# Gate-unit splitting of four more weight groups in a transformer layer, kept in DRAM as two parts and loaded as operands

## The chip, the cores and the metric

One NeuronCore of a Trainium2 chip runs the whole layer as one program. The metric is device time in microseconds from launch to end, lower is better. The kernel before ran three times: 2187.90, 2187.95 and 2191.87 us, median 2187.95.

## The reference

One layer of a decoder trunk, all in float32, sequence 1024, width 1024:

```
x = x + 1/2 * SwiGLU_1(RMSNorm(x))
z = RMSNorm(x) @ W_in           # u, v, c_q, c_kv, k_rope, q_mem, gates A, B, C
A: u * (tril(W_s) layernorm(v) + b), in chunks of 128
B: causal attention, 8 heads; q = rmsnorm(c_q) @ w_uq, k and v = rmsnorm(c_kv) @ w_ukv
C: cross-attention to 256 memory tokens, 4 heads
x = x + (sum_i sigmoid(gate_i) * (y_i @ W_branch_i)) @ W_out
x = x + 1/2 * SwiGLU_2(RMSNorm(x))
```

`w_uq` is 384 x 768, `w_ukv` 256 x 1024, each `W_branch` 512 x 1024.

## The kernel before, in words

**Three products for one.** TensorE takes its operands in a reduced form of float32 (`F32R`). To keep the accuracy, every operand x is split into two parts, hi = x rounded to that form and lo = x - hi, and `mm3` (L145) multiplies hi by hi, hi by lo and lo by hi into one PSUM bank. The split (`split`, L133) is a copy on ScalarE (L134) and a subtraction on VectorE (L135). Every weight that is fetched raw goes through it once before it can be used; `load` and `convert` (L103, L107) do this for a fetched weight in pieces of 512 columns: the DMA brings the raw weight into a `raw` buffer (three of them, each 128 x 1024), and the split writes it into a pair of `whi` and `wlo` buffers (five of each).

**The stages.** First feed-forward; the gates' product h @ W_in (`Gates.run`, L1767); the mixer (`mixer`, L926: spatial gating, memory attention, up-projections, causal attention); then branch B, the output projection and the second feed-forward.

**The gates.** W_in is worked off in 19 units, each a seven-product Strassen scheme of 7 x 4 x 3 = 84 matmuls of 512 columns. A unit fetches one quad of weight tiles (`fetch`, L1415: two DMAs of 512 KB, and two buffers for the sums that VectorE builds, L1422), splits them (`weights`, L1436), keeps the first product as p1 (a ScalarE copy, L1483), and writes its outputs to DRAM. The buffers come from two pools: ten `x4` and eleven `w4`, each 128 x 1024 floats; units with an even number take four `x4`, units with an odd number two `x4` and two `w4` from unit 3 on. Between units other weights are already prepared: after units 4 to 7 the sums of W_out (`out_sums`, L1687), which go to DRAM as hi and lo parts and are later loaded as operands (the same is done for the memory's keys and values after unit 8, and for the memory query in units 14 and 15). `out_sums` takes the four buffers of the next turn, two loads, four GpSimd subtractions (L1696 to L1699), one split and three stores.

**The mixer.** Value rows (`value_rows`, L571) are multiplied with W_v, whose four pairs of wide buffers stay in use until the last row. `gating` (L620) mixes them, `mem_attention` (L711) and branch A's output product (`branches`, L550) interleave with it. `latent` (L430) reads the latent rows through `raw`. `qkv` (L450) then multiplies with w_uq and w_ukv, interleaved with steps of branch C, and `attention` (L789) begins with the rest of branch C. `branches` takes one weight per 128 output columns: 128 x 4 x 128 floats, 256 KB, loaded raw and split by one copy and one subtraction of 512 columns. Branch A's parts go to a `whi` and a `wlo` buffer, branch C's into halves of one `raw` buffer (`half_pair`, L546), so that branch C holds one `raw` buffer to stage and one for the parts; for its last two weights VectorE does the copy too. `qkv` loads w_uq in three fetches and w_ukv in two; together they hold all five pairs of wide buffers.

**The order.** All DMAs around the change are issued by SyncE (SP) in one queue, in order: a transfer whose buffer or operand is not ready holds all behind it. In the gates TensorE's order is written out by hand for the first units and kept as the program has it for the rest; SP, ScalarE, VectorE and GpSimd are ordered by a planner that simulates the timeline and assigns the buffers. In the mixer the planner orders TensorE as well. The last keys and queries of the causal attention go to DRAM (L530, L533) and come back as pairs (`pair_half`, L539) before TensorE can transpose them (L406).

Of the kernel before, what the change touches and what calls it, by code (L numbers as in the profile page):

```python
# [9 lines left out]
F32 = mybir.dt.float32  # L10
F32R = mybir.dt.float32r
# [3 lines left out]
ALU = mybir.AluOpType  # L15
AXX = mybir.AxisListType.X

P = 128
D = 1024
S = 1024  # L20
DT = D // P
# [5 lines left out]
H = 8  # L27
NOPE = 64
ROPE = 32
QK = NOPE + ROPE  # L30
VD = 64
QR = 384
# [13 lines left out]
MEM_AT = 8  # L46
# [3 lines left out]
class Kernel:  # L50
# [399 lines left out]
    def qkv(self, cq, ckv, krs, krr, eps, rc, aside):  # L450


        nc, a, tc = self.nc, self.a, self.tc
        half = ROPE // 2
        wq = self.load(a["mla_w_uq"])
        wk = [self.load(a["mla_w_ukv"][g]) for g in range(2)]
        T = 2
        vv = []
        with tc.tile_pool(name="qkvp", bufs=2) as p:
# [16 lines left out]
            for i0 in range(0, NT, T):  # L476
                q = p.tile([P, T, H, QK], F32, name="q")
                k = p.tile([P, T, H, QK], F32, name="k")
                ss = self.stat("qk_ss", 2 * T * H).rearrange("p (a t h) -> p a t h", a=2, t=T)
                for t in range(T):  # L480
                    i = i0 + t
                    c = slice(i * P, i * P + P)
# [60 lines left out]
            eng.dma_start(t, d[h // 2][:, half * NT // 2:(half + 1) * NT // 2])  # L543
            self.pair[n, half] = t

    def half_pair(self):  # L546
        t = self.raw(F32R)
        return t[:, :512], t[:, 512:]

    def branches(self, br, yt, sink, halves, rooms=(), first=3):  # L550

        nc, a, w, rooms = self.nc, self.a, {}, list(rooms)

        steps = [(dt, hf) for hf in halves for dt in range(first)]
        for dt, hf in steps + [(dt, hf) for dt in range(first, DT) for hf in halves]:
            if dt not in w:
                w[dt] = self.load(
                    a["w_branch"][br, dt], rooms.pop(0) if rooms else None,
                    copy=nc.vector.tensor_copy if br == 2 and dt >= DT - 2 else None)
            sig = self.row()  # L560
            nc.sync.dma_start(sig, self.sig[br * DT + dt][:, hf])
            b = self.bank()
            self.branch(b, w[dt], yt, hf)
            sink(dt, hf, sig, b)
            yield
# [360 lines left out]
    def mixer(self, norm):  # L926
        nc, tc, a = self.nc, self.tc, self.a
        dt = lambda shape, n: self.dram.tile(shape, F32, name=n)
        self.pair = {}
        self.qd = dt([H // 2, P, NT, 2 * QK], "qd")  # L930
        self.kd = dt([H // 2, P, NT, 2 * QK], "kd")
        md, mc = dt([DT, 2, P, 512], "md"), dt([DT, 2, P, 512], "mc")
        pairs = lambda n: [tuple(x[:, i] for x in norm.op[n][p]) for p in range(2) for i in range(2)]
        h = [pairs("b12") + pairs("b22"), pairs("b11") + pairs("b21")]

        def sink_a(d, f, sig, ps):
            nc.vector.tensor_tensor(sig, sig, ps, op=ALU.mult)
            nc.sync.dma_start(md[d, f], sig)

        def sink_c(d, f, sig, ps):  # L940
            m = self.row()
            nc.sync.dma_start(m, md[d, f])
            nc.vector.tensor_tensor(sig, sig, ps, op=ALU.mult)
            nc.gpsimd.tensor_tensor(sig, sig, m, op=ALU.add)
            nc.sync.dma_start(mc[d, f], sig)

        ln_g, ln_b = self.row(), self.row()
        nc.sync.dma_start(ln_g, a["sg_ln_g"].partition_broadcast(P))
        nc.sync.dma_start(ln_b, a["sg_ln_b"].partition_broadcast(P))
        with tc.tile_pool(name="mem", bufs=1) as p:  # L950
            w = self.convert(self.w_v)
            kt, vv = self.mem_operands(p)
            qt, nr, query = self.mem_query(p)
            query(0)
            vs = [[], []]
            sw = self.gating_weights()
            ya, aside = self.gating(sw, vs)
            branch_a = self.branches(0, ya, sink_a, (1, 0), first=4)
            fill, mix = (lambda x=x: next(x) for x in (branch_a, aside))
            for f, q, also in ((1, 0, {}), (1, 1, {}), (0, 0, {}), (0, 1, {d: mix for d in (1, 2, 4, 6, 7)})):  # L960
                x = self.value_rows(f, q, h, w, also)
                self.value_norm(x, q, ln_g, ln_b, vs[f])
            lead = [(fill, fill), (fill, mix, mix), (mix, fill), (mix, mix, fill)]
            branch_c = self.mem_attention(
                kt, vv, qt, nr, query, lead, branch_a, lambda yc: self.branches(
                    2, yc, sink_c, (0, 1), [self.half_pair] * DT, first=1))
        with tc.tile_pool(name="pairs", bufs=1) as self.pairs:
            with tc.tile_pool(name="lt", bufs=1) as self.lp:
                z = self.latent()
                for _ in range(2):  # L970
                    next(branch_c)
                vv = self.qkv(*z, branch_c)
            yb = self.attention(vv, branch_c)
        return yb, mc
# [335 lines left out]
class OpNorm:  # L1310
# [45 lines left out]
    def part(self, p):  # L1356
        for piece in self.pieces(p):
            piece()
# [34 lines left out]
class Seven:  # L1393
# [42 lines left out]
    def weights(self, f, part):  # L1436

        k = self.k
        a1, a2, sa, sb = self.quad[f]
        src, names = {  # L1440
            "a": (a1, ("a11", "a12")), "s": (sa, ("s2", "s1")), "t": (sb, ("s3", "s4")),
            "l": (a2[:, :1], ("a22",))}[part]
        n = len(names)
        hi, lo = (k.wide(x).rearrange("p (a w) -> p a w", a=2)[:, :n] for x in ("whi", "wlo"))
        k.split(hi, lo, src)
        return {x: (hi[:, i], lo[:, i]) for i, x in enumerate(names)}
# [166 lines left out]
class Gates(Seven):  # L1613
# [73 lines left out]
    def out_sums(self, u, rooms):  # L1687
# [15 lines left out]
        nc.sync.dma_start(k.wo["hi", q][:, :, i], a1)  # L1703
        nc.sync.dma_start(k.wo["lo", q][:, :, i], a2)

    def square_sums(self, n, half, d):

        k = self.k
        sq = k.row()
        self.nc.scalar.activation(sq, d, ACT.Square)  # L1710
        fresh = self.bank is None
        if fresh:
            self.bank = k.bank()

        def go():
            for t in range(4 * half, 4 * half + 4):
                at = t * MH + n - QM
                self.nc.tensor.matmul(
                    self.bank[:, at:at + 1], sq[:, t % 4 * P:t % 4 * P + P], k.ones,
                    start=fresh and t == 4 * half, stop=True, skip_group_check=True)  # L1720

        self.sums_todo.append(go)
# [44 lines left out]
    def run(self, x1d, r0):  # L1767


        k, norm, x4, w4 = self.k, self.norm, self.k.x4, self.w4  # L1770
        last = UNITS - 1
        k.mkv = {n: [k.dram.tile([P, D], F32, name=f"{n}{i}") for i in range(2)] for n in ("mk", "mv")}
        k.wo = {
            (n, q): k.dram.tile([P, 2, 2, 512], F32, name=f"wo_{n}{q}") for n in ("sum", "hi", "lo") for q in range(2)}
        k.zsums = k.const.tile([P, NT * MH], F32, name="zsums")
        k.g_mq = k.const.tile([P, 1], F32, name="g_mq")
        k.after(self.nc.vector.tensor_scalar(k.g_mq, k.mq_g, -(MD ** -0.5), None, op0=ALU.mult), k.last)
        E = mybir.EngineType
        with k.tc.manual_schedule(engines={E.PE, E.DVE, E.Activation}):
            self.units((0, 1), extra=2, kinds=(k.bank, k.single, k.single, k.bank, k.bank), late=1, turn=2)  # L1780
        with k.tc.manual_schedule(engines={E.PE}):
            for f in range(3, last + 1):
                self.fetch(f, [x4, w4, x4, w4] if (last - f) % 2 else [x4] * 4)
                if f == last:
                    more = k.fetch(k.a["w_v"], [x4, x4])
                    k.w_v = chain([next(more) for _ in range(2)], more)
                    for p in range(2):
                        norm.t.t[0, p] = w4()
                        self.nc.sync.dma_start(norm.t.t[0, p], x1d[0, p])
                    norm.s[0] = k.norm_scale(r0)  # L1790
                    for p in range(2):
                        norm.norm(0, p)
                self.unit(f)
                turn = [x4, w4, x4, w4], [x4] * 4
                if MEM_AT > f >= MEM_AT - 4:
                    self.out_sums(f - MEM_AT + 4, turn[(last - f + 1) % 2])
                if f == MEM_AT:
                    self.memory(turn[(last - f) % 2] + turn[(last - f + 1) % 2])
                if 2 * f >= CQ and self.bank is not None:
                    self.flush()  # L1800
                    nc = self.nc
                    nc.vector.tensor_copy(k.zsums, self.bank[:, :NT * MH])
                    self.bank = None
            for p in range(2):
                norm.put("b12", p, norm.t.t[0, p])
# [425 lines left out]
```

## Time and profile before

| | |
|---|---|
| median of three runs | 2187.95 us (2187.90 to 2191.87) |
| profiled execution, first to last instruction (span) | 2187.2 us; what lies around it was not recorded apart, the median of the runs is 0.75 us above it |
| TensorE busy | 2163.2 us (99%), 10153 matmuls |
| VectorE, ScalarE, GpSimd busy | 1560.4 (71%), 908.5 (42%), 219.0 us (10%) |
| DMA | 315.8 MB, mean 144 GB/s |
| granted TensorE clock | 1.00 over the span |
| gates' units 3 to 18 | about 700 to 1056 us |
| mixer up to the causal attention | about 1036 to 1290 us |

A row of a group names the line, the engine, the operation, the tiles written and read, the count, the busy time and the mean of one in ns; what follows the second bar is the idle time ahead of it and what ended it. In a row by stage each engine's busy time has its instruction count behind it. Many matmuls overlap, so busy TensorE means that it never ran dry, not that it ran at its peak.

### The profile page before, as it was taken

Reading aid. Unit: us, or ns where it says so; the run is one execution under the profiler, and the core shown is the slowest. Engines: PE = TensorE matmul, PEld = TensorE weight load, DVE = VectorE, ACT = ScalarE, POOL = GpSimd, SP = SyncE. Lnnn points to the kernel's source line nnn. Section 1 sums busy time; section 2 is a strip of 40 time slices with the busy share of each in tenths; the row PEclk is TensorE's granted clock in tenths of the full one; section 3 lists DMA queues with packets and bytes.
Section 4 is the critical chain, followed back from the end, with each engine's and each line's share of the span. In section 5 each row is a group of like instructions: output and inputs, shape, how many; then the busy total and the mean of one; then the engine's idle time right before and its main releaser. Section 6 shows DMA issues by size and latency. Waiting matters only on the chain.

```text
span 2187.2 us, 27190 instructions
## 1 busy us (share of the span) xinstructions
PE 2163.2 (99%) x10153; PEld 1797.6 (82%) x10153; DVE 1560.4 (71%) x2285; ACT 908.5 (42%) x1375; POOL 219.0 (10%) x234
## 2 busy tenths in 40 slices
PE   8999999999999999999999999999999999999999
PEld 4788888888888888888888889988888888888887
DVE  7965666569889657556588788898985665556964
ACT  5432223233445435433266549844532322224332
POOL 0011212110000220000000431200001111211000
PEclk9999999999999999999999999999999999999999
DMA  4232333384432673334356661166243333338442
GB/s 155 88 124 91 112 101 114 107 329 151 151 125 81 227 260 106 135 135 170 118 173 198 207 202 35 54 229 238 82 135 96 97 115 92 116 130 317 140 140 97
DMA packets 131925, 315.80 MB, mean 144 GB/s; under 512 B 14608, under 2 KB 23056, under 8 KB 131792
## 3 DMA queue, kind: packets, MB, share of 16 engines
q1 hardware_dynamic: 129392, 311.69, 42.6%
q10 hardware_dynamic: 2400, 2.36, 0.3%
q8 instruction: 80, 1.31, 0.3%
q14 instruction: 53, 0.43, 0.1%
HBM read 216.35 MB, written 97.65 MB: 144 GB/s over the span
## 4 chain that ended last, share of the span: by engine, by line
PE 87%; DVE 9%; DMA 2%; ACT 1%; issue 1%; POOL 0%; SPq 0%; ACTq 0%; DVEq 0%; POOLq 0%
PE one L148 15%; PE one L150 15%; PE one L149 15%; PE bank L148 10%; PE bank L149 10%; PE bank L150 10%; PE mm L148 2%; DVE wlo L135 2%; PE mm L150 2%; PE mm L149 2%; PE bank L864 1%; PE bank L879 1%; DVE h L135 1%; PE bank L880 1%; PE bank L406 1%
## 5 line engine op out<-in xcount | busy, mean ns | idle before, releaser
L134 ACT CAST whi<-x 128x1024 fp32r<-128x1024 f32 (+1 forms) x213 | 200.5, 946 | 510.4 <-PE one L149 213.1
L1457 DVE TENSOR_TENSOR t<-t,one 128x512 f32<-128x512 f32 x149 | 102.3, 687 | 245.0 <-PE one L150 244.8
L135 DVE TENSOR_TENSOR wlo<-x,whi 128x1024 fp32r<-128x1024 f32 (+1 forms) x213 | 233.3, 1099 | 42.5 <-ACT whi L134 42.5
L148 PE MATMUL bank<-h,whi 128*128 128x512 f32 x592 | 231.1, 391 | 1.1 <-ACT t L1483 0.7
L149 PE MATMUL bank<-h,whi 128*128 128x512 f32 x592 | 230.5, 389 | 0.0
L150 PE MATMUL bank<-h,wlo 128*128 128x512 f32 x592 | 230.4, 390 | 0.0
L135 DVE TENSOR_TENSOR wlo<-w,whi 128x1024 fp32r<-128x1024 f32 (+1 forms) x153 | 168.8, 1117 | 75.3 <-ACT whi L134 75.1
L134 ACT CAST whi<-w 128x1024 fp32r<-128x1024 f32 (+1 forms) x153 | 142.4, 954 | 167.0 <-PE one L149 104.9
L148 PE MATMUL one<-h,whi 128*128 128x512 f32 x528 | 206.6, 391 | 1.7 <-ACT t L1483 1.2
L150 PE MATMUL one<-h,wlo 128*128 128x512 f32 x528 | 205.6, 389 | 0.5 <-DVE wlo L135 0.5
L149 PE MATMUL one<-h,whi 128*128 128x512 f32 x528 | 205.5, 389 | 0.0
L148 PE MATMUL one<-w,whi 128*128 128x512 f32 x464 | 180.7, 390 | 0.3 <-DVE t L1457 0.3
L150 PE MATMUL one<-w,wlo 128*128 128x512 f32 x464 | 180.6, 389 | 0.0
L1971 POOL TENSOR_TENSOR raw<-raw 128x512 f32<-128x512 f32 x36 | 75.6, 2100 | 882.5 <-DVE raw L1829 652.2
L1457 DVE TENSOR_TENSOR raw<-t,one 128x512 f32<-128x512 f32 x130 | 89.1, 686 | 88.1 <-PE one L150 81.1
L149 PE MATMUL one<-w,whi 128*128 128x512 f32 x380 | 147.9, 389 | 0.0
L148 PE MATMUL one<-whi 128*128 128x512 f32 (+1 forms) x371 | 143.9, 388 | 0.0
L149 PE MATMUL one<-wlo,whi 128*128 128x512 f32 (+1 forms) x371 | 143.7, 387 | 0.0
L150 PE MATMUL one<-whi,wlo 128*128 128x512 f32 (+1 forms) x371 | 143.7, 387 | 0.0
L148 PEld LDWEIGHTS bank<-h,whi 128*128 128x128 f32 x592 | 111.1, 188 | 24.6 <-ACT t L1483 1.2
L150 PEld LDWEIGHTS bank<-h,wlo 128*128 128x128 f32 x592 | 111.1, 188 | 23.2
L149 PEld LDWEIGHTS bank<-h,whi 128*128 128x128 f32 x592 | 111.2, 188 | 22.7
(424 smaller groups left out, 4784.8 us busy)
## 6 DMA issues: line engine op xcount, KB each, us to landing
x<-in_ffn_w_gu_dram SPq DMA_DIRECT2D x76, 512.0 KB, 4.4
w<-tdt SPq DMA_DIRECT2D x40, 512.0 KB, 3.8
tdb<-raw SPq DMA_DIRECT2D x64, 256.0 KB, 2.0
gate<-raw SPq DMA_DIRECT2D x32, 512.0 KB, 3.5
w<-tdb SPq DMA_DIRECT2D x30, 512.0 KB, 6.9
h<-in_ffn_w_down_dram SPq DMA_DIRECT2D x28, 512.0 KB, 6.5
x<-in_w_in_dram SPq DMA_DIRECT2D x26, 512.0 KB, 6.1
tdt<-w SPq DMA_DIRECT2D x44, 256.0 KB, 2.0
```

The costliest lines, as they stand in the source:

```text
L134: (copy or self.nc.scalar.copy)(hi, src)
L135: return (eng or self.nc.vector).tensor_tensor(lo, src, hi.bitcast(F32), op=ALU.subtract)
L148: mmul(out, s[0], m[0], start=first, stop=False, **kw)
L149: mmul(out, s[0], m[1], start=False, stop=False, **kw)
L150: self.last = mmul(out, s[1], m[0], start=False, stop=last, **kw)
L406: nc.tensor.transpose(b[:m, k * P:(k + 1) * P], s, self.ident)
L864: nc.tensor.transpose(b[:, at:at + P], prs[t][:, kk * P:(kk + 1) * P], self.ident)
L879: nc.tensor.matmul(o, w, pt[0], start=n == 0, stop=False)
L880: nc.tensor.matmul(o, w, pt[1], start=False, stop=n == len(pts) - 1)
L1457: return self.nc.vector.tensor_tensor(out, x, y, op=ALU.add)
L1971: sub = lambda d, x, y: eng.tensor_tensor(d, x, y, op=ALU.subtract)
```

## The change

The weights of branches A and C, w_uq and w_ukv are no longer split in the mixer. After each of the units 9 to 15 up to two `part` steps load a raw piece (128 x 2 x 512 or 128 x 2 x 384), copy it on ScalarE to hi, subtract on GpSimd to lo, and store both to DRAM (`wparts`). There are 13 pieces: four of branch A, four of branch C, three of w_uq, two of w_ukv, in this order. They take the buffers of the turn of the unit that they follow, two per piece. In the mixer `branches` loads a 512 KB tile with both parts side by side, for branch A in turn into a `whi` and a `wlo` buffer, for branch C into a `raw` buffer; `qkv` loads hi and lo of each piece into a `whi` and a `wlo` buffer. `half_pair` goes, and so does VectorE's copy for the last two weights of branch C.

```
     def qkv(...):
-        wq = self.load(a["mla_w_uq"])
-        wk = [self.load(a["mla_w_ukv"][g]) for g in range(2)]
+        def weights(n, width):
+            t = [self.wide(x, F32)[:, :2 * width].rearrange("p (c w) -> p c w", c=2) for x in ("whi", "wlo")]
+            for i, x in enumerate(t):
+                nc.sync.dma_start(x, self.wparts[n][:, i])
+            return [tuple(x[:, c].bitcast(F32R) for x in t) for c in range(2)]
+
+        wq = [x for q in range(QR // P) for x in weights(("q", q), H * QK // 2)]
+        wk = [weights(("k", g), 512) for g in range(2)]
...
     def branches(self, br, yt, sink, halves, rooms, first=3):
...
             if dt not in w:
-                w[dt] = self.load(
-                    a["w_branch"][br, dt], rooms.pop(0) if rooms else None,
-                    copy=nc.vector.tensor_copy if br == 2 and dt >= DT - 2 else None)
+                t = rooms.pop(0)()
+                nc.sync.dma_start(
+                    t.rearrange("p (a w) -> p a w", a=2), self.wparts[br, dt // 2][:, :, dt % 2])
+                t = t.bitcast(F32R)
+                w[dt] = [
+                    tuple(t[:, x + k * P:x + (k + 1) * P] for x in (0, 512)) for k in range(4)]
...
-            branch_a = self.branches(0, ya, sink_a, (1, 0), first=4)
+            wide = [lambda x=x: self.wide(x, F32) for x in ("whi", "wlo")]
+            branch_a = self.branches(0, ya, sink_a, (1, 0), wide * (DT // 2), first=4)
...
-                    2, yc, sink_c, (0, 1), [self.half_pair] * DT, first=1))
+                    2, yc, sink_c, (0, 1), [self.raw] * DT, first=1))
...
+    def part(self, n, src, a, b):
+        k, nc = self.k, self.nc
+        a, b = (t()[:, :, :src.shape[-1]] for t in (a, b))
+        nc.sync.dma_start(a, src)
+        hi, lo = b.bitcast(F32R), a.bitcast(F32R)
+        nc.scalar.copy(hi, a)
+        nc.gpsimd.tensor_tensor(lo, a, b, op=ALU.subtract)
+        for i, t in enumerate((b, a)):
+            nc.sync.dma_start(k.wparts[n][:, i], t)
...
     def run(self, x1d, r0):            # of Gates
+        k.wparts, parts = {}, []
+        for n, src in chain(
+                (((br, q), k.a["w_branch"][br, 2 * q:2 * q + 2].rearrange("c p k w -> p c (k w)"))
+                 for br in (0, 2) for q in range(DT // 2)),
+                ((("q", q), k.a["mla_w_uq"][:, 2 * q:2 * q + 2]) for q in range(QR // P)),
+                ((("k", g), k.a["mla_w_ukv"][g]) for g in range(2))):
+            k.wparts[n] = k.dram.tile([P, 2, *src.shape[1:]], F32, name=f"wp_{n[0]}{n[1]}")
+            parts.append((n, src))
...
+                if f > MEM_AT:
+                    rooms = list(turn[(last - f + 1) % 2])
+                    while parts and rooms:
+                        self.part(*parts.pop(0), rooms.pop(0), rooms.pop(0))
```

More of the change, by code (lines that the diff above doesn't have):

```diff
@@ L544, in pair_half, with branches @@
             self.pair[n, half] = t
[L546 to L552, printed above, removed]
+    def branches(self, br, yt, sink, halves, rooms, first=3):
+        nc, w, rooms = self.nc, {}, list(rooms)
         steps = [(dt, hf) for hf in halves for dt in range(first)]
```

## The prediction

> **What bounds the kernel now.** I read the head of the page first, then the busy time by stage, then TensorE's waits in the two stages that the change touches.
>
> ```profile
> span 2187.2 us, 27190 instructions
> PE 2163.2 (99%) x10153; PEld 1797.6 (82%) x10153; DVE 1560.4 (71%) x2285; ACT 908.5 (42%) x1375; POOL 219.0 (10%) x234
> ```
>
> TensorE is idle for 2187.2 - 2163.2 = 24.0 us of the whole span, so no change that leaves the matmuls as they are can gain more. The view by stage gives for each stretch the busy time and count of PE, PEld, DVE, ACT and POOL, then the granted clock, the DMA share and GB/s.
>
> ```profile
> 200.00:250.00 50.00, 50.00 (x222) 41.39 (x221) 30.80 (x40) 14.18 (x18) 8.94 (x5) 1.00 0.33 104
> 780.00:799.00 19.00, 18.26 (x81) 15.07 (x81) 11.58 (x14) 8.50 (x12) 5.81 (x4) 1.00 0.64 236
> 922.00:941.00 19.00, 19.00 (x86) 15.72 (x85) 9.73 (x13) 7.93 (x10) 0.00 (x0) 1.00 0.25 85
> 1100.00:1150.00 50.00, 45.93 (x296) 40.50 (x295) 41.57 (x79) 31.75 (x84) 0.00 (x0) 1.00 0.53 178
> 1150.00:1250.00 100.00, 100.00 (x546) 88.80 (x546) 82.58 (x161) 59.05 (x128) 22.83 (x29) 1.00 0.62 195
> 1250.00:1300.00 50.00, 47.67 (x249) 40.55 (x248) 37.51 (x71) 17.87 (x38) 23.03 (x27) 1.00 0.78 257
> 1185.00:1190.00 5.00, 5.00 (x33) 4.61 (x32) 3.90 (x10) 2.40 (x6) 0.00 (x0) 1.00 1.04 358
> 1275.00:1280.00 5.00, 3.91 (x20) 3.02 (x19) 2.30 (x4) 1.26 (x2) 2.97 (x3) 1.00 0.99 347
> ```
>
> A gates' unit lasts 19 us. In an ordinary one (922:941) TensorE has no gap, GpSimd is empty and DMA is a quarter busy: that is the room into which the work goes. The mixer, from which it comes, loses TensorE time only in 1100:1150 (50 - 45.93 = 4.07) and 1250:1300 (2.33). In 1150:1250, where the query and key-value weights and most of branch C's are split, VectorE is busy for 82.58 of 100 us and TensorE still has no gap. The prize is at most 4.07 + 2.33 = 6.4 us. TensorE's waits from 1060 to 1300 (waiting line, releaser, total us, times, longest) name the causes:
>
> ```profile
> PE bank L643 <- ACT t L633: 1.9, 4, 0.6
> PE mm L148 <- ACT mpr L732: 1.8, 3, 1.0
> PE bank L148 <- DVE t L943: 1.1, 1, 1.1
> PE mm L150 <- DVE x L141: 1.0, 1, 1.0
> PE bank L148 <- DVE t L937: 0.3, 1, 0.3
> PE bank L406 <- DMA aq<-qd: 0.2, 1, 0.2
> ```
>
> None of them names a weight split (ACT whi or DVE wlo read from raw). The first two, 3.7 us, are the round trips of the spatial gating and of the memory softmax in 1100:1150. The splits stand indirectly behind the third, fourth and sixth, 2.3 us, at the turn into the causal attention.
>
> **The change part by part: what leaves the mixer.** Groups by shape from 1056 to 1300, ScalarE's, then VectorE's:
>
> ```profile
> L134 ACT CAST whi<-raw 128x512 fp32r<-128x512 f32 x17 | 10.3, 622 | 24.4 <-DMA raw<-in_w_v_dram 10.7 <-PE mm L150 4.4 <-DMA raw<-in_w_branch_dram 4.1
> ...
> L134 ACT CAST raw<-raw 128x512 fp32r<-128x512 f32 x6 | 3.7, 621 | 11.1 <-PE bank L150 6.2 <-DMA raw<-in_w_branch_dram 3.2 <-DVE wlo L135 1.7
> ```
>
> ```profile
> L135 DVE TENSOR_TENSOR wlo<-raw,whi 128x512 fp32r<-128x512 f32 x18 | 12.2, 686 | 11.5 <-ACT whi L134 11.5
> ...
> L135 DVE TENSOR_TENSOR raw<-raw 128x512 fp32r<-128x512 f32 x8 | 7.4, 931 | 3.2 <-ACT raw L134 3.1
> ...
> L134 DVE CAST raw<-raw 128x512 fp32r<-128x512 f32 x2 | 1.4, 716 | 0.0
> ```
>
> Branch A has 8 pieces of 512, the up-projections 7 (and three remainders of 256, left out here), branch C 8 (the raw<-raw rows). ScalarE loses 15 x 0.622 + 3.7 = 13.0 us, VectorE 15 x 0.686 + 7.4 + 1.4 = 19.1 us. Almost all of it lies where TensorE has no gap, and is worth nothing there. At the turn it is worth something:
>
> ```profile
> 1263.36 0.68 DVE L135 TENSOR_TENSOR raw<-raw 128x512 fp32r<-128x512 f32 x1
> ```
>
> ```profile
> 1279.47 1.66 DVE L135 TENSOR_TENSOR raw<-raw 128x512 fp32r<-128x512 f32 x1
> 1281.05 0.74 DVE L141 SCALAR_TENSOR_TENSOR x<-bank,a_gq,x 96x512 fp32r<-96x512 f32 x1
> ```
>
> ```profile
> 1268.24 0.61 DVE k L525
> ...
> 1269.34 6.40 DMA kd<-k
> ...
> 1276.37 6.15 DMA aq<-qd
> ...
> 1282.58 0.51 PE bank L406 x3
> ```
>
> The split at 1279.47 holds L141, for which TensorE waits 1.0 us. Without it the next thing late is the landing of aq at 1282.52, which ends a chain through L525, kd and aq. So the 1.0 comes back only as far as that chain moves forward, and the split at 1263.36 in it is about 0.6 us. Add part of the 1.1 behind L943, whose operand came late through a DMA stretch with a share of 0.99. Against it stands the traffic: a branch C step now loads both parts, 512 KB for 256 KB, though it needs one raw buffer instead of two and can be fetched further ahead. Bounds: -2.3 (all three waits) to +2.3 (three loads' extra 262 KB at 347 GB/s, 0.76 us each, if none moves ahead). I take **-1.0**, nearer to the named waits than to the traffic.
>
> **The start of the up-projections.** Five loads of 2.23 MB become ten of 4.46 MB into the wide buffers. In 1185:1190 the DMA share is already 1.04 at 358 GB/s, so 2.23 MB more are 6.2 us if they start where they start now. They no longer stage through raw, which the latents' rows occupy until then, so those whose wide buffers are free can start earlier; the last pair waits for branch A's last weights, as now. Bounds 0 (TensorE has no gap here, so no gain) to +6.2; I take **+0.5**.
>
> **What the gates' units get.** Thirteen parts, two after each of the units 9 to 15 (the last has one). A part is one load and two stores on SP's queue, one ScalarE copy and one GpSimd subtraction of 1024 columns (768 for the query weights): 39 DMA issues more on SP. The nearest rows are those of the w_out sums after units 4 to 7, which take the same four buffers, two loads and three stores: the chain of waits at 760, then GpSimd and VectorE in order of time.
>
> ```profile
> 760.17 7.50 DMA x<-in_w_out_dram
> ...
> 767.83 1.95 POOL x L1696
> ...
> 772.31 0.53 SPq L1701
> ...
> 772.89 5.65 DMA x<-in_w_in_dram
> ...
> 778.61 1.05 ACT whi L134
> ```
>
> ```profile
> 772.36 1.29 POOL L1698 TENSOR_TENSOR x<-x,x 128x512 f32<-128x512 f32 x1
> ```
>
> ```profile
> 772.55 1.65 DVE L135 TENSOR_TENSOR wlo<-x,whi 128x512 fp32r<-128x512 f32 x1
> ```
>
> ScalarE gets 13 x about 1.05 = 13 us, GpSimd 13 x 2 x 1.29 = 33 us (an estimate from the 512 columns), each spread over 133 us in which they are busy for 7.93 and 0 of 19. The throughput fits. DMA goes up by 2 x 3 x 0.524 MB per 19 us = 166 GB/s, to 251 over the 85 of 922:941, just above the 236 of 780:799. What can cost time is the order. The store of the low part waits on SP for GpSimd, and behind it stands the next unit's weight fetch (L1419); ScalarE's copy waits for the part's load, and behind it stand the gate's copies (L1483) and weight splits (L134), for which TensorE waits. In the rows above SP held the fetch behind L1701 until 772.31, the weights landed at 778.5, ScalarE's split came at 778.61, and TensorE lost 19 - 18.26 = 0.74 us. That happened in one of four such units; it was one of the two odd units among the four, whose first weight tile takes the only x4 buffer of its fetch and so waits for a buffer that a sum's tiles held. Bounds: 0, as in 200:250, where the up-projection's units have 8.94 us of GpSimd subtractions and no gap on TensorE, to 7 x 0.74 = 5.2. Below nothing is excluded, since TensorE has no gap there to give. I take four odd units, every second one stalled: **+1.5**. Where this cover goes, the fetch is next, as in rival 2.
>
> Sum, on the profiled execution: 2187.2 - 1.0 + 0.5 + 1.5 = 2188.2 of span. The median of the runs, 2187.95, lies 0.75 above that span, so **2188.95, forecast as 2189.0**: no difference that can be told. About 0.2%, 4.4 us, is what a measurement of this kernel can tell from no change.
>
> **The rivals.** *1. Faster.* The mixer is ordered by a planner, and SP is blocked in it by branch A's loads, which wait for raw:
>
> ```profile
> 1073.53 19.17 SPq L100 DMA_DIRECT2D raw<-in_w_branch_dram  x2
> 1092.75 0.42 SPq L627 DMA_DIRECT2D t<-gate  x1
> ```
>
> The gating's operand (L627) stands behind them. If it comes earlier, the gating steps move into the value rows, the 1.9 of L643 goes, and with the full 2.3 at the turn and 0.8 of the softmax wait that is -5.0: 2183.0. Against it: the first weights still wait for wide buffers which the value rows hold, and neither wait names a DMA.
>
> *2. Slower, by the queue.* Place: SP and ScalarE in units 10 to 16. The price is the 0.74 in every one of the seven, 5.2, with the turn's gain gone to traffic: 2187.95 + 5.2 + 0.5 + 0.5 = 2194.2. It decides from the point at which the next unit's weights land too late for ScalarE's copy of p1. That copy has one product of 12 matmuls, 12 x 18.26 / 81 = 2.7 us, before TensorE writes its bank again. For it: two chains a unit instead of one, ScalarE waiting on loads directly. Against it: three of four out-sum units lost nothing.
>
> [...] VectorE's 512-column split at 772.55 began 0.19 us after a GpSimd subtraction of 1.29 and took 1.65, against the 0.686 of its group. TensorE lost nothing by that, so a delay of about 0.96 is covered. A 2.58 us subtraction can hold it for 2.2, 1.2 beyond what is shown covered; with VectorE busy in some 0.6 of the time, 13 x 0.6 x 1.2 = 9.4 us: 2197.4. [...] 200:250 speaks against the price.
>
> *4. Slower, at the up-projections:* the 6.2 us of extra traffic all exposed, without the other costs: 2194.
>
> *That the change does nothing for the mixer* (weights land when they were split before) lies within the forecast.
>
> **How the numbers follow.** Forecast 0.53, rival 1 0.20, rival 2 0.17, rival 3 0.06, rival 4 0.04. The likeliest case alone spans 2185 to 2192. The range takes in rivals 1, 2 and 4 with something beyond, and leaves out most of 3 and a gain of the full 6.4: 2182 to 2197. Faster by over 0.2% is rival 1, 0.20; within 0.2% 0.53; slower 0.17 + 0.06 + 0.04 = 0.27.
>
> **What would show it.** Gates: stretches of 19 us from 865 to 1000 with PE at 19.00 (forecast: two with some 0.7 missing), POOL at 5 in each, DMA share near 0.7; rivals 2 and 3 show as TensorE's waits on L1483 or on DVE wlo in each unit, SP's fetch behind a part's store, and L135 at over 2 us. Up-projections: TensorE's waits on DMA of whi or wlo. Turn: no raw<-raw on VectorE, L141 right after its releaser, aq landing within 1 us of its old distance to L525. 1100:1150: PE near 45.9 if I am right, over 48 for rival 1. The forecast is wrong if the mixer's TensorE order changes so far that other waits, in the attention too, add up to more than 4 us.

## The result, and the profile after

The changed kernel takes 2203.09 us (median of four runs, 2197.53 to 2204.39), beside 2188.54 for the kernel before (median of four): 1.0057 times as long, 95% interval 1.0042 to 1.0072. The change makes the kernel slower by 14.6 us, and the forecast of 2189.0 with its range up to 2197 was wrong. One execution among those below, of *a_only*, took 2797.20 us at a mean granted clock of 0.728 and is left out of its median. The head of the profile after:

```profile
span 2202.4 us, 27261 instructions
PE 2169.7 (99%) x10153; PEld 1803.1 (82%) x10153; DVE 1554.8 (71%) x2257; ACT 906.2 (41%) x1364; POOL 247.9 (11%) x247
```

VectorE and ScalarE have a little less to do, as forecast. TensorE's 10153 matmuls are the same, but it idles 2202.4 - 2169.7 = 32.7 us instead of 24.0, and it is busy for 6.5 us longer with the same work. 8.7 + 6.5 = 15.2 us is the whole difference of the two spans. The view by stage (length, busy time and count of PE, PEld, DVE, ACT and POOL, granted clock, DMA share, GB/s) says where:

```profile
865.00:884.00 19.00, 16.95 (x68) 13.56 (x67) 18.03 (x31) 9.95 (x13) 6.69 (x4) 0.91 0.83 298
884.00:903.00 19.00, 19.00 (x90) 15.82 (x89) 14.40 (x15) 10.64 (x14) 6.35 (x3) 1.00 1.02 371
922.00:941.00 19.00, 19.00 (x85) 15.75 (x84) 10.87 (x12) 9.36 (x13) 3.70 (x2) 1.00 0.74 270
1100.00:1150.00 50.00, 43.98 (x252) 38.03 (x252) 40.53 (x74) 31.43 (x76) 0.00 (x0) 0.97 0.49 165
1150.00:1200.00 50.00, 47.04 (x295) 42.20 (x293) 31.85 (x56) 25.44 (x64) 0.00 (x0) 0.97 0.57 196
1250.00:1300.00 50.00, 47.39 (x218) 39.71 (x217) 31.32 (x61) 13.56 (x29) 21.90 (x27) 0.97 0.86 284
```

In the gates only 865:884, the first unit after parts were begun, loses TensorE time (19.00 - 16.95 = 2.05); the others are full, even with the DMA engines at a share of 1.02. The mixer loses 6.02 instead of 4.07 in 1100:1150 and 2.96 instead of nothing in 1150:1200. What is left of the 8.7 us lies in small amounts elsewhere. In all four losing stretches (1250:1300, which lost 2.33 before, now loses 2.61) the granted clock is below 1.00, which it never was in these stretches before. That is the longer busy time: until its last 2 us the trace has four spells of 3.41 us at half clock, at 872.81, 1128.81, 1180.01 and 1296.07, each worth 1.7 us of work. The next view shows, for three of them, the 3.41 us before a spell, in which a gap lies, and then the spell:

```profile
869.40:872.81 3.41, 1.36 (x7) 0.82 (x6) 3.29 (x14) 2.37 (x4) 0.00 (x0) 1.00 0.42 172
872.81:876.23 3.42, 3.42 (x9) 2.68 (x10) 3.42 (x7) 0.78 (x1) 0.00 (x0) 0.50 0.96 279
1125.40:1128.81 3.41, 1.41 (x13) 1.21 (x11) 3.41 (x5) 3.41 (x11) 0.00 (x0) 1.00 0.46 148
1128.81:1132.23 3.42, 3.42 (x17) 3.42 (x17) 3.11 (x5) 3.42 (x10) 0.00 (x0) 0.50 0.00 0
1176.60:1180.01 3.41, 1.34 (x12) 1.10 (x11) 3.41 (x8) 3.16 (x9) 0.00 (x0) 1.00 0.70 226
1180.01:1183.43 3.42, 3.42 (x18) 3.42 (x17) 2.57 (x5) 1.93 (x6) 0.00 (x0) 0.50 0.25 78
```

So these gaps, 2.05, 2.00 and 2.07 us of idle TensorE, cost nearly double, with the 1.7 us of the spell behind each. TensorE's waits in 1060 to 1310 (waiting line, releaser, total us, times, longest), and the one of 860 to 880:

```profile
PE bank L648 <- ACT t L638: 2.8, 4, 1.5
PE mm L148 <- ACT mpr L737: 2.8, 3, 2.0
PE mm L148 <- DVE h L135: 2.1, 1, 2.1
PE bank L406 <- DMA t<-gate: 1.4, 1, 1.4
PE mm L150 <- DVE x L141: 1.2, 1, 1.2
...
PE one L148 <- DVE t L1463: 2.0, 1, 2.0
```

The first two are the gating and the memory softmax, as before, but longer (1.5 for 0.6, 2.0 for 1.0). The third and the last are new.

### The profile page after: what moved, and what is told of

It is laid out like the page before. It is cut to its first block, busy times and chain, and to the rows that moved or that the text cites. A ratio compares the mean times of both kernels' runs of the same rounds, so it can differ in the third digit from the quotient of the medians.

```text
span 2202.4 us, 27261 instructions
## 1 busy us (share of the span) xinstructions
PE 2169.7 (99%) x10153; PEld 1803.1 (82%) x10153; DVE 1554.8 (71%) x2257; ACT 906.2 (41%) x1364; POOL 247.9 (11%) x247
## 4 chain that ended last, share of the span: by engine, by line
PE 85%; DVE 10%; DMA 2%; issue 1%; ACT 1%; POOL 0%; SPq 0%; DVEq 0%; ACTq 0%; POOLq 0%
PE one L148 15%; PE one L149 15%; PE one L150 15%; PE bank L148 10%; PE bank L149 10%; PE bank L150 10%; DVE wlo L135 2%; PE mm L148 2%; PE mm L149 2%; PE mm L150 2%; PE bank L869 1%; DVE h L135 1%; PE bank L884 1%; PE bank L885 1%; PE bank L406 1%
## 5 line engine op out<-in xcount | busy, mean ns | idle before, releaser
L148 PE MATMUL bank<-h,whi 128*128 128x512 f32 x560 | 219.0, 391 | 2.0 <-ACT t L1489 1.7
L149 PE MATMUL bank<-h,whi 128*128 128x512 f32 x560 | 217.9, 389 | 0.0
L150 PE MATMUL bank<-h,wlo 128*128 128x512 f32 x560 | 217.8, 389 | 0.0
L148 PEld LDWEIGHTS bank<-h,whi 128*128 128x128 f32 x560 | 105.1, 188 | 24.6 <-ACT t L1489 2.2
L150 PEld LDWEIGHTS bank<-h,wlo 128*128 128x128 f32 x560 | 105.1, 188 | 22.0
L149 PEld LDWEIGHTS bank<-h,whi 128*128 128x128 f32 x560 | 105.2, 188 | 21.4
```

The costliest lines, as they stand in the source:

```text
L148: mmul(out, s[0], m[0], start=first, stop=False, **kw)
L149: mmul(out, s[0], m[1], start=False, stop=False, **kw)
L150: self.last = mmul(out, s[1], m[0], start=False, stop=last, **kw)
```

## The experiments

All ratios are to the kernel before, with 95% intervals.

**1. Gates or mixer?** Two runs take one half each. *gates_only* keeps the parts and gives the mixer its old loads back:

```
-        wq = [x for q in range(QR // P) for x in weights(("q", q), H * QK // 2)]
+        wq = self.load(a["mla_w_uq"])          # wk, branches A and C likewise
```

> The thirteen parts are made and stored in the gates' units, but nothing reads them: the mixer loads and splits its weights as before. Theory P (places): the loss lies at a few named places. In the gates it is the first unit with parts, where the two subtractions on GpSimd meet the memory's normalisation on VectorE: TensorE stops for 2.2 us there and then runs 3.4 us at half its clock, 1.7 us more. So 3.9 us above the kernel before, about 2192 to 2193, with the later units without a gap. Theory Q (queues and traffic): the extra issues and bytes cost in every unit, and all of the 14.5 us come from the gates: about 2202. Theory M (mixer alone): no loss in the gates: 2188 to 2189.

Measured: 2192.32 us, 1.0012 (1.0003 to 1.0021). *mixer_only* has the mixer of the change:

```
+            first = {0: (0, 0), 2: (0, 0), "q": ("q", 0), "k": ("k", 0)}[n[0]]
+            if n != first:
+                k.wparts[n] = k.wparts[first]; continue
-                if f > MEM_AT:
+                if f > MEM_AT + 2:
```

> Three of the thirteen parts are made, in units 11 and 12; every piece of branches A and C reads the parts of branch A's first two pieces, every query piece those of the first and every key-value piece those of the first, so the output is not the reference's. The mixer's loads, buffers and order of work are those of the change, and unit 9 has no parts. Theory P: the mixer's own share of the loss stays, two or three more spells at half clock and the larger gaps between 1100 and 1190 us: about 10 us above the kernel before, 2198. Theory Q: nothing of the loss is in the mixer: 2188 to 2190.

Measured: 2199.11 us, 1.0040 (1.0028 to 1.0053). The two add up to 1.0052, near the 1.0057 of the change. Most of the loss is in the mixer; theory Q, the traffic and the queues in the gates, falls.

**2. What the gates pay for.** In the changed kernel the order of time at 862 us, VectorE's rows, then GpSimd's, then TensorE's:

```profile
863.08 2.68 DVE L1435 TENSOR_TENSOR x<-x,x 128x512 f32<-128x512 f32 x1
865.68 2.89 DVE L1440 TENSOR_TENSOR x<-x 128x512 f32<-128x512 f32 x1
868.49 0.16 DVE L157 TENSOR_SCALAR rs_i<-hn_v 128x8 int32<-128x8 int32 x1
...
871.90 0.68 DVE L1463 TENSOR_TENSOR t<-t,one 128x512 f32<-128x512 f32 x1
```

```profile
862.80 5.21 POOL L1719 TENSOR_TENSOR x<-x,w 128x1024 fp32r<-128x1024 f32 x2 [69.05 <-ACT w L1718]
```

```profile
870.21 0.39 PE L150 MATMUL one<-h,wlo 128*128 128x512 f32 x1
872.64 0.66 PE L148 MATMUL one<-h,whi 128*128 128x512 f32 x1 [2.05 <-DVE t L1463]
```

Two fetch sums that take 0.68 alone (line 1438 at 868.63) took 2.68 and 2.89 while the subtractions of two parts ran on GpSimd. Behind them stood the chain of small operations that normalises the memory's rows, and behind that the addition that frees TensorE's bank. This stretch had less room than the ordinary one before the change as well, 13.53 us of VectorE for 9.73; its row in the kernel before:

```profile
865.00:884.00 19.00, 19.00 (x85) 15.61 (x84) 13.53 (x29) 8.09 (x12) 0.00 (x0) 1.00 0.47 167
```

*from10* starts the parts one unit later, *gates_only_dve* is gates_only with the subtraction on VectorE:

```
-                if f > MEM_AT:
+                if f > MEM_AT + 1:                                      # from10
-        nc.gpsimd.tensor_tensor(lo, a, b, op=ALU.subtract)
+        nc.vector.tensor_tensor(lo, a, b, op=ALU.subtract)              # gates_only_dve
```

> The change with the parts begun one unit later, so that none is made while the memory's rows are normalised. Theory P: the gap of 2.2 us at 870 us and the half clock after it go, 3.9 us below the changed kernel, about 2199, with VectorE's operations in unit 10 under 1 us where they met the subtractions in 2.7 and 2.9. [...] Theory Q: unchanged, 2203, or worse, since the last part moves one unit on, nearer to its use.

> All thirteen parts made from unit 9 on and read by nothing, as in the run of the gates alone, but with the part's subtraction on VectorE. If VectorE and GpSimd keep each other out (VectorE's operations of 2.7 and 2.9 us at 863 us beside GpSimd's subtractions of 2.4 and 2.9), the gap of 2.2 us at 870 us goes and the time is 2189 to 2190, 2 to 3 us below that run, the subtraction itself taking 1.2 to 1.4 us on VectorE. If it is the memory's chain and the part's ScalarE copy that make the gap, it stays: 2192. If VectorE in unit 9 becomes too full, the gap grows: 2193 or more.

Measured: from10 2200.78 us, 1.0043 (1.0030 to 1.0057), its stretch 865:884 at 18.41 of 19. GpSimd subtracts for 5.54 us in it and VectorE is busy for 17.49, but TensorE lost only 0.6 us there. gates_only_dve 2189.30 us, 1.0001 (0.9993 to 1.0010):

```profile
865.00:884.00 19.00, 19.00 (x85) 15.73 (x84) 18.06 (x34) 9.83 (x14) 0.00 (x0) 1.00 0.99 359
```

With 13 subtractions more on VectorE, which is then busy for 18.06 of 19 us, the gates lose nothing. Their loss came with the subtractions on GpSimd, beside which VectorE's two sums took 2.68 and 2.89 us for 0.68, in the one stretch where VectorE had a chain of small operations to carry and the least time in hand.

**3. Which weights?** Each run makes only one group of parts, from unit 10 on, the rest loaded and split as before:

```
+            if n[0] not in (0,):            # a_only; (2,) c_only; ('q', 'k') up_only
+                continue
```

> Only branch A's four pairs of weights are made as parts, in units 10 and 11; branch C and the up-projections are loaded raw and split as before. Theory A: the mixer's loss in 1100 to 1190 us comes from branch A alone. Its weights no longer pass raw and need no split, so the planner, which orders TensorE there, puts its steps elsewhere among the memory attention, and the round trips through ScalarE and VectorE that they covered lie open: the stretches 1100:1150 and 1150:1200 lose 3 to 8 us more than before, the turn at 1290 us is as before, and the time is 2193 to 2198. Theory U: the up-projections' loads, which no longer pass raw, are what lets the latents' rows in early; then this run is at 2189 to 2191.

> Only branch C's four pairs of weights are made as parts, in units 10 and 11. Theory A: nothing changes in 1100 to 1190 us. At the turn (1275 to 1295 us) two things work against each other: the splits on VectorE are gone (the 1.0 us wait for line 141), and each step loads 512 KB for 256 KB. If the traffic decides, the spell at half clock and the longer wait of line 406 for its transfer are here, 2 to 4 us, 2191 to 2193; if the splits decide, 1 to 2 us faster than before, 2187 to 2189, with 1 us for the gates taken in.

> Only the query and key-value weights are made as parts (five), in units 10 to 12. Theory A: these weights are late in any case for nothing, TensorE has no gap there, so the time is that of the kernel before plus about 1 us for the gates: 2189 to 2190. Theory U: the loads' leaving raw lets the latents' rows in early and brings the loss of 1100 to 1190 us: 2194 to 2198.

Measured: a_only 2197.76 us, 1.0038 (1.0025 to 1.0051); c_only 2190.17, 1.0008 (1.0000 to 1.0017); up_only 2190.99, 1.0013 (1.0004 to 1.0021), the last two with TensorE waits of 0.5 and 1.7 us in the gates (c_only has TensorE busy for 18.37 of 19 us in 865:884) and the kernel before's waits in 1100 to 1200. The mixer's loss comes with branch A alone. The complement, *cup_dve*, has the parts of C and of the up-projections, subtracted on VectorE:

> Parts for branch C and the up-projections only (nine, from unit 9 on), subtraction on VectorE, branch A as before. Every place of loss that the runs have shown is avoided: the gates as before, 1100 to 1190 us as before. At the turn the two runs of one part each lost 2.6 us where the kernel before lost 3.5. Expected 2186.5 to 2189, not to be told from the kernel before, or faster by up to 2 us. If both parts together crowd the transfers at the turn, a spell at half clock appears there, 2190 to 2192.

Measured: 2188.31 us, 1.0002 (0.9993 to 1.0011). Its stages, 1100 to 1200 and the turn:

```profile
1100.00:1150.00 50.00, 45.91 (x293) 40.41 (x292) 41.56 (x78) 31.42 (x84) 0.00 (x0) 1.00 0.54 179
1150.00:1200.00 50.00, 50.00 (x308) 44.93 (x307) 37.71 (x74) 28.95 (x65) 2.58 (x6) 1.00 0.67 241
1250.00:1300.00 50.00, 48.16 (x239) 40.72 (x239) 31.15 (x62) 15.29 (x34) 21.67 (x27) 0.97 0.82 272
```

Nine of the thirteen parts are free, and bring nothing: at the turn TensorE is busy 0.5 us longer than before, part of it at half clock in this execution, and *gates_only_dve*, whose mixer is the one before, has 48.33 us there.

**4. What branch A's weights set off.** SyncE's loads of the latents' rows, before, then after (count, duration, first and last start):

```profile
L416 SPq DMA_DIRECT2D raw<-gate x5: 319/319/383, 1151.7 to 1173.2; - x5
```

```profile
L416 SPq DMA_DIRECT2D raw<-gate x5: 319/320/378, 1071.8 to 1181.5; - x5
```

Before, three of branch A's weights lay in the three raw buffers from 1099 us until their splits (1148.6 to 1170.6 us). The change leaves these buffers empty, so three of the latents' rows come 80 us earlier. The early rows go with branch A's parts and with no others, as the same view of a_only and of c_only shows (in up_only and cup_dve the first starts at 1153.1 and 1151.9):

```profile
L416 SPq DMA_DIRECT2D raw<-gate x5: 319/320/378, 1068.2 to 1179.4; - x5
L416 SPq DMA_DIRECT2D raw<-gate x5: 319/320/320, 1152.8 to 1174.4; - x5
```

Their work on ScalarE then falls into the memory attention. Two places in the changed kernel:

```profile
1125.38 1.14 ACT L138 ACTIVATE x<-raw,c_mla_cq_norm 128x1024 fp32r<-128x1024 f32 x1
1126.42 0.55 ACT L737 ACTIVATE mpr<-mm,m_mx,m_nr 128x256 f32<-128x256 f32 x1
...
1174.14 0.35 ACT L134 CAST h<-mm 128x256 fp32r<-128x256 f32 x1
1176.85 0.63 ACT L353 ACTIVATE t<-raw 128x512 f32<-128x512 f32 x1 [2.35 <-DMA md<-t]
...
1177.85 0.38 ACT L134 CAST h<-mm 128x256 fp32r<-128x256 f32 x1
```

At 1125 a scaling of 1.14 us stands ahead of the memory softmax, and the longest wait for the softmax is 2.0 instead of 1.0 us. At 1174 ScalarE waits 2.35 us for one of the six row buffers t, which a store of branch A (md<-t) has to free. Behind it stands the last copy of a value product out of its PSUM pair (h<-mm), and TensorE needs that pair for the next value product:

```profile
1176.47 1.03 PE L791 MATMUL bank<-ident,mpr 128*128 128x128 f32 x8
1179.58 0.39 PE L148 MATMUL mm<-whi,mv_hi 128*128 128x256 f32 x1 [2.07 <-DVE h L135]
```

The next runs undo one thing at a time in the whole change. *latent_late* holds the latents' work on ScalarE until the second value product:

```
-            acc[f] = self.norm_feed(acc[f], raw[:, c], 512)
-        self.split_gain(dst[0], dst[1], raw, gain)
+            acc[f] = self.norm_feed(acc[f], raw[:, c], 512, mark=self.value_end)
+        self.split_gain(dst[0], dst[1], raw, gain, mark=self.value_end)
```

> The change with one order added: ScalarE's scaling and squaring of the latents' rows (lines 138 and 353) wait until the second value product of the memory attention, where they stood before the change. Theory P, cause 1: they slipped in between the memory softmax's exponentials and the gating's evacuations because their rows came earlier, and grew two gaps of TensorE by about 1 us each, one of which set off a spell at half clock (1.7 us): 3.5 to 4 us below the changed kernel, about 2199. Rival: these gaps stand on VectorE's chain or on weights still to land, and ScalarE's order is only filling: no change, 2203, or slower by up to 2 us if the latents are then late for the up-projections.

Measured: 2205.20 us, 1.0067 (1.0054 to 1.0079). 1100:1150 came back as expected, and the loss went to the next stretch:

```profile
1100.00:1150.00 50.00, 46.28 (x288) 40.62 (x288) 37.71 (x72) 27.77 (x73) 0.00 (x0) 1.00 0.53 176
1150.00:1200.00 50.00, 44.75 (x273) 40.19 (x271) 35.94 (x63) 28.66 (x66) 0.00 (x0) 0.93 0.59 193
```

*sub_dve* is the whole change with the subtraction on VectorE, the control for what follows. *hand* adds TensorE's written order in the memory attention's turns, *hand_late* both orders:

```
+            with self.tc.manual_schedule(engines={mybir.EngineType.PE}):
                 for i in range(4):
                     turn(i)
```

> The whole change, with the part's subtraction on VectorE instead of GpSimd. From the run of the gates alone, which lost 3 us with GpSimd and nothing with VectorE: 3 to 4 us below the changed kernel, about 2199 to 2200, all that is left being the mixer's. Control for the next two.

> As the run before it, and TensorE's order in the memory attention's four turns (lines 770 to 787 of the changed kernel) is the one in which they are written: transposes, one step of branch A, scores, value product, one step, and so on. Theory O: the loss at 1177 us is one of order. The planner, with branch A's weights in hand earlier, spent one step of A more ahead of the first value product, so that the last value products follow their transposes with nothing between. With the written order each value product has 12 matmuls of A (2.7 us) ahead of it, and the gap of 2.2 us with its spell at half clock goes: 3 to 4 us below the control, about 2196. Theory W: the gap comes from VectorE's and ScalarE's other work (latents' rows) and comes back at another place: 2199 or more.

> As the run before it, and the latents' rows are scaled and squared only after the second value product. Theory O with the early rows as the second cause: both of the mixer's losses in 1100 to 1200 us are gone, 2190 to 2192, the turn at 1290 us being all that is left. If the two causes share a third one (the whole chain through ScalarE and VectorE is too full there), it stays at 2196 or above, with the gap of 4.2 us at 1172 us that the run with late rows alone showed.

Measured: sub_dve 2197.23 us, 1.0044 (1.0031 to 1.0057); hand 2197.24, 1.0043 (1.0030 to 1.0056); hand_late 2197.40, 1.0050 (1.0036 to 1.0064). TensorE's waits in 1140 to 1200, of sub_dve, then of hand:

```profile
PE mm L148 <- DVE h L135: 1.9, 1, 1.9
PE bank L148 <- DVE wlo L135: 0.6, 1, 0.6
```

```profile
PE bank L148 <- DMA whi<-wp: 1.6, 1, 1.6
PE bank L148 <- DVE wlo L135: 0.9, 3, 0.5
```

The written order takes the gap away and meets others. In 1100 to 1140 TensorE waits 5.4 us for the gating (line 648) where the control waits 2.8. After that A's later weights have not landed: before the change three of them were staged in raw, and in the changed kernel their loads start at 1155.6, 1167.6, 1175.1 and 1183.8 us, when a wide buffer comes free. hand_late lacks the gap of 4.2 us that was its other outcome, but in 1140 to 1200 it waits 3.1 us for splits on VectorE, 2.2 for the softmax and 1.1 for a weight. The four *staged* runs put two of them back into raw, as parts:

```
-            branch_a = self.branches(0, ya, sink_a, (1, 0), wide * (DT // 2), first=4)
+            branch_a = self.branches(0, ya, sink_a, (1, 0), wide * 2 + [self.raw] * 2 + wide, first=4)
```

> The whole change with the subtraction on VectorE, and branch A's fifth and sixth weights loaded, as parts, into two raw buffers instead of wide ones, so that they lie there before 1105 us; the latents' rows have one raw buffer until then. TensorE's order stays the planner's, in which the last value products still follow their transposes directly. Theory S (staging is the common cause): the short wait for a weight at 1160 us goes, the latents' rows come later because two raw buffers are taken, and 1100:1200 loses 10 to 12 us instead of the control's 15 (2197.2): 2193 to 2195. Theory O (order alone makes the gap at 1177 us): that gap stays, 2195 to 2197. Theory L (ScalarE and VectorE are too full): 2197.

> As the run before it, with TensorE's written order in the four turns. Theory S: neither the gap at 1175 us nor the wait of 1.8 us for a weight at 1182 us that came in its place is there; left are the first latents' row among the softmax and the gating, 1 to 2.5 us: 2191 to 2194. Theory L: a gap of 2 us or more appears at another place in 1140 to 1185 us, 2196 or more.

> As the run staged, with the latents' rows scaled and squared only after the first value product (about 1147 us) and the planner's order. Theory S: 1100:1150 is as in the kernel before (6.6 us against the control's 9.9), 1150:1200 loses 2 to 5 us as in staged: 2191 to 2195. Theory L: the work put off comes down on 1150 to 1180 us and the loss moves there, as in the two runs with late rows: 2197 or more.

> Staged weights, written order and late rows together. Theory S: all three losses of the mixer are gone, 1100:1200 loses about 8 us as in the kernel before, and the time is 2188 to 2190. Theory L: 2195 or more. If it lies between, the gap with the largest length says which of the three is still there.

Measured: staged 2200.25 us, 1.0046 (1.0034 to 1.0059); staged_hand 2194.82, 1.0023 (1.0013 to 1.0034); staged_late0 2196.28, 1.0031 (1.0020 to 1.0042); staged_hand_late0 2192.51, 1.0019 (1.0010 to 1.0028). Alone staging gains nothing, and the gap before the value product grew to 3.8 us. The three together win back 4.7 of the control's 8.6 us, so theory S holds for about half. In the last run TensorE's largest wait in 1140 to 1200 is a new one of 2.0 us, while ScalarE waits in 1155 to 1178 for a latents' row still to land:

```profile
PE bank L794 <- DVE t L945: 2.0, 1, 2.0
```

```profile
ACT x L138 <- DMA raw<-gate: 2.8, 2, 2.1
```

*own_rows* and *own_rows_staged_hand* take the squares off the row buffers, the first in sub_dve, the second in staged_hand:

```
-        sq = self.row()[:, :w]
+        sq = (rows or self.row)()[:, :w]        # rows: a pool of its own, for the latents
```

> The whole change with the subtraction on VectorE (control 2197.2), and the latents' squares written to a pool of their own instead of the row buffers t. That pool lies over the memory attention's room, so the squares come after its last product. Theory R (ScalarE stands in its queue at the squares, for a row buffer): no wait of line 353 for md<-t, the gap of 2.1 us at 1172 us and its spell at half clock go, 1150:1200 loses 1 to 2 us instead of 5.2, and the time is 2193 to 2194.5. Theory O (order alone): the gap stays, since the planner's order of TensorE is the same there: 2196 to 2198. If the squares are then late for the up-projections, a new gap of 2 to 5 us stands at 1195 to 1210 us.

> The same pool in the run staged_hand (2194.8): two of A's weights staged in raw buffers, the written order of TensorE. Theory R: the gap of 2.4 us at 1173 us goes, 2191 to 2192.5, what is left being the first latents' row among the softmax (1 to 1.5 us at 1121 us, and a spell in some executions) and the turn. Rival: that gap is ScalarE waiting for a latents' row still to land (raw<-gate, 2.2 us in that run), which this does not change: 2194 to 2195.

Measured: 2205.11 us, 1.0072 (1.0059 to 1.0084), and 2203.52, 1.0066 (1.0052 to 1.0080). TensorE in own_rows:

```profile
1171.82 1.03 PE L792 MATMUL bank<-ident,mpr 128*128 128x128 f32 x8
1173.10 0.39 PE L148 MATMUL mm<-whi,mv_hi 128*128 128x256 f32 x1 [0.24 <-DVE h L135]
...
1189.83 1.41 PE L426 MATMUL bank<-ones,sqr 128*128 128x1 f32 x6 [4.38 <-DVE sqr L358]
```

TensorE's order is the control's at this place, and the wait is 0.24 instead of 1.9 us. So the gap was ScalarE standing at the squares, as theory R has it, and not the order alone, which theory O took for it. But the squares, now late, hold up the sums (L426) by 4.4 us, and the whole is slower. No version beat the kernel before.

## Why the prediction was wrong

**The failing step is the mixer's removal of branch A's splits**: "Almost all of it lies where TensorE has no gap, and is worth nothing there", and with it the check "1100:1150: PE near 45.9 if I am right". It was 43.98, and 47.04 where 50.00 had been. I priced the instructions that go and not the buffers that they held. Branch A's stay in raw had been holding back the latents' rows; without it their ScalarE work comes in between the softmax, the gating and the splits. The prediction says of raw that branch A's loads "wait for raw" and that "the latents' rows occupy" it, not that these rows would come into it sooner. Its last sentence named the case, other waits in the mixer of more than 4 us, and gave it no chance of its own. Of the order named there the runs bear out little: own_rows has the control's order without the gap. Rival 1 fell by the argument that stands against it there: SyncE no longer stands at the raw buffers, but two of A's loads wait for wide ones until 1095.38 us, and the gating's operand behind them starts at 1096.62, against 1092.75 before.

**The clock was left out of the sum.** Four spells at half clock make 6.5 of the 15.2 us. The waits quoted from the trace before were 1.1 us at most, and it has no price for a longer one.

**The gates: +1.5 forecast, 1.0012 or 2.6 us measured, by the other mechanism.** GpSimd's throughput was right (3.7 to 6.7 us in the stretches shown, 5 forecast). DMA's was added to the emptiest unit: 251 GB/s forecast, 371 measured in 884:903, which moved 166 before. The queue behind a part's store cost nothing: the stretches from 884 us on are full. The loss was rival 3's, held at 0.06: VectorE's two sums took 2.0 and 2.2 us longer beside GpSimd's subtractions (2.68 and 2.89 for 0.68). The second of the two ended at 868.57 us, 0.56 after the subtractions (862.80 + 5.21). My price of it was wrong in kind. I spread it evenly, 13 x 0.6 x 1.2 us, while VectorE's slack absorbed every meeting but those in 865:884, where the memory's normalisation left too little: later operations of VectorE took 2.77, 2.53 and 2.67 us beside a subtraction (at 883.32, 901.01 and 991.45), and TensorE is full from 884 to 998 us. The forecast took 922:941 for all seven units.

**The start of the up-projections, +0.5,** is right in size: 1200:1250 has TensorE at 50.00 of 50 after the change too, with up_only and cup_dve showing no wait for these weights.

**The turn, -1.0,** is not borne out. c_only has TensorE busy for 48.30 in 1250:1300, against 47.67, but gates_only_dve has 48.33 with the mixer as it was, so this difference says nothing of the weights. In the whole change the wait for line 141 is still there (1.2 us), line 406 waits 1.4 for a transfer, and a spell at half clock follows. Why line 141 stays late was not tried.

**The step from span to time, +0.75,** set the median of the runs against the span of one profiled execution. Where a run's time and span are both on record, 1.7 to 2.1 us lie between them (2204.19 and 2202.4 for the changed kernel). That error of about 1 us is small beside the 14.6.

**What is open.** The causes in the mixer do not add up: early rows, A's unstaged weights and the planner's order each give nothing when undone alone, and undone together about half; the wait for a row buffer could only be taken away at the price of late sums. For the other half, about 4 us, the profile of that run names a wait on VectorE at 1171 us and the turn, but neither was taken away by itself.

## What to carry to other kernels

Before you take a staging buffer's user away, ask who is next in line for the buffer: here the latents' rows came 80 us earlier, a scaling of 1.14 us on ScalarE then stood ahead of the memory softmax, and TensorE's longest wait for the softmax went from 1.0 to 2.0 us. Price moved GpSimd work at the one place where VectorE carries a chain for TensorE, not by its average load; here the same subtraction was free on a VectorE busy for 95% of the stretch (18.06 of 19 us in gates_only_dve). Where TensorE is the bound, count a new gap of about 2 us as up to nearly 4, as here, where 1.7 us at half clock came on top of 2.05, 2.00 and 2.07.

## What the runs showed of the hardware

**The granted clock fell in spells of 3.41 us.** The four spells of the changed kernel last 3.41 us each and start 256.00, 51.20 and 116.06 us apart, which are 75, 15 and 34 times 3.4133 (256.00 / 75) to within 0.01 us. A fifth starts 904.53 us after the fourth, 265 times that, at 2200.60, 1.8 us before the end of the span. So the time ahead of a spell is read here in windows of 3.41 us. The length of a gap alone does not tell what follows: behind the gap of 2.05 us in the changed kernel at 870 us the clock was halved, behind a wait of 2.0 us at the same place in gates_only it was not. That the windows lay otherwise in gates_only is my estimate; in the one that I put around that wait TensorE is busy for 1.63 us, beside 1.36 in the changed kernel's:

```profile
870.60:874.01 3.41, 1.63 (x7) 1.37 (x8) 3.35 (x8) 2.73 (x4) 0.00 (x0) 1.00 0.51 160
874.01:877.43 3.42, 2.78 (x13) 1.96 (x12) 3.42 (x6) 1.39 (x2) 0.00 (x0) 1.00 0.94 319
```

In from10 a window with 1.65 us of busy time kept its clock, and one with 1.55 lost it:

```profile
1133.48:1136.90 3.42, 1.55 (x10) 1.12 (x11) 3.41 (x5) 2.32 (x4) 0.00 (x0) 1.00 0.61 172
1136.90:1140.31 3.41, 3.41 (x13) 2.72 (x12) 2.51 (x4) 0.79 (x2) 0.00 (x0) 0.50 0.84 257
1174.43:1177.85 3.42, 1.65 (x14) 1.42 (x13) 3.27 (x8) 3.39 (x10) 0.00 (x0) 1.00 0.60 214
1177.85:1181.26 3.41, 3.41 (x30) 3.33 (x29) 2.61 (x5) 2.70 (x9) 0.00 (x0) 1.00 0.24 89
```

In seven traces eleven windows at full clock were read that a spell followed. TensorE was busy in them for 1.12, 1.34, 1.36 and 1.41 us (the changed kernel), 1.23 (staged_hand_late0), 1.55 (from10), 1.57 (cup_dve), 1.67 (staged_hand), 1.68 and 1.83 (mixer_only) and 2.04 (latent_late, at 1290.84). Windows with 1.63 us (gates_only), 1.65 and 1.69 (from10), 2.05 (staged_hand_late0, at 1120.57) and 2.35 (the changed kernel, at 1135.64) kept the clock. So each of those with 1.57 us or less lost it, and from 1.63 to 2.05 it went either way; what decides there stays open. A spell of 3.41 us at half clock costs some 1.7 us. The times of one kernel's runs go with their mean clock: of cup_dve's eleven runs the eight with a mean clock of 1.000 took 2188.09 to 2188.58 us and the three with 0.999 took 2189.25 to 2190.69, and the changed kernel's fastest run of 2197.53 had a mean clock of 0.999 against 0.996 or 0.997 in the others.

**VectorE beside subtractions on GpSimd.** In the changed kernel VectorE operations of 128x512 took 2.53 to 2.89 us beside a subtraction on GpSimd (at 863.08, 865.68, 880.64, 883.32, 901.01 and 991.45), for 0.68 to 0.69 without. Not every one did: line 1463 at 913.57 took 0.69 within a subtraction that lasted from 912.76 to 915.20. With all thirteen subtractions on VectorE (gates_only_dve) no wait of TensorE shows in 850 to 1000 us.
